# Hybrid convolution and delta-rule layer on one core: q, k, v stored by chunk, spreads by transposes, the last projection pairs product by product, early masks, longer steps for three conv norms

## The chip, the cores and the metric

The kernel runs on one core of one Trainium2 chip. The metric is the device time of one execution in microseconds (us). All engines run at once, each through its own queue in order: TensorE (PE), VectorE (DVE), ScalarE (ACT), GpSimd (POOL) and SyncE (SP), which here issues nearly all DMAs. Arithmetic is float32; large products are made from operands split into a high and a low part.

## The reference

For 1024 tokens of width 1024 the layer computes

```
h = x + 0.5 * swiglu_ffn(rmsnorm(x), ffn1)             # width 2816
u = rmsnorm(h) @ w_mix_in                              # 3 x 512 conv, q k v z of 4 heads x 128, b, a
y_conv = rmsnorm_by_group_of_64(cb * conv3(cc * ch))
q, k, v = silu(conv4(q k v));  q, k = l2norm(q), l2norm(k)
beta = sigmoid(b);  g = -exp(A_log) * softplus(a + dt_bias)
o = gated_delta_rule(q, k, v, g, beta)                 # by chunks, a triangular solve in each, a scan over chunks
y_gdn = rmsnorm(o) * silu(z)
h = h + concat(y_conv, y_gdn) @ w_mix_out
h = h + 0.5 * swiglu_ffn(rmsnorm(h), ffn2)
out = rmsnorm(h)
```

## The kernel before

Activations lie transposed: 128 channels on the partitions, 512 tokens (a half, `hf`) on the free axis. A product step `mm3` (L191) issues three matmuls of 128x128 by 128x512, high by high, high by low and low by high, into one PSUM bank, then calls `tick` (L184), which runs what was put off by `later(n, f)` until n such steps have gone by. `split` (L99) makes the two parts, the high one on ACT (L103) and the low one on DVE (L104).

The stages are the first feed-forward block, the projection to q, k and v, the mixer, and the second feed-forward block. The two blocks and the q, k, v projection use a seven-product scheme (Strassen-Winograd): a `Pair` (L323) makes two neighbouring column tiles for both halves, with products p1 and p2 in its head and p6, p5, p7, p4, p3 in `body` (L381). Each of them is 12 matmuls. p7, p4 and p3 go on in PSUM banks that p6 and p5 began, and DVE reads the bank between two of them. `all_pairs` (L426) puts the bodies of pairs 0, 1 and of pairs 2, 3 in the order product by product (p6 of one, p6 of the other, p5 of one, ...), and those of the pairs from 4 on one after the other; the q, k, v projection has six pairs, so its pairs 4 and 5 (tiles 8, 9 and 10, 11: v) come singly. Tasks have a load, a preparation and a run; preparations go 4 and loads 9 tasks ahead.

When a pair's tile is done, `conv4` (L824) makes its causal convolution over four tokens: a scaling on ACT (L826), three DVE operations (L828), a SiLU on ACT (L830), and a store to `qkv_dr` in DRAM (L831). Its second half and v tiles 10 and 11 are done in the mixer by `late_convs` (L1319): 14 convolutions, each in two steps, a load and the convolution.

The mixer has 8 chunks of 128 tokens. `build(c)` (L984) loads k and q of the chunk from `qkv_dr` (L988), makes the decay matrices by matmuls of a mask with `r0` (L993 on POOL, L1013 and L1016 on PE), and in later steps transposes k, q and v on PE by `flip` (L925, L929). v is loaded (L1050) one step ahead of its transpose (L1065). `solve(g)` (L1076) inverts the diagonal blocks of four chunks on DVE (L1094, L1098); `finish(c)` and `scan(c)` end each chunk. Between such steps `pump` (L1332) issues product steps of the z and short-convolution projections (`rest`), 2.7 for each step of a build. `drive` (L1362) runs the builds of chunks 0 to 3 three steps apart with one step of `late_convs` after each of their steps, then those of chunks 4 and 5 with three steps of `solve(0)` after each.

A conv norm (`conv_norm`, L1224) squares a finished tile, has `reduce` 7 product steps later sum it by groups of 64 (four PE matmuls, L1231, a scaling on DVE, L1234, and a power on POOL, L1237), and `scale` 8 steps after that widen the factors on ACT (L1242), spread them over the partitions by four PE matmuls with the identity (L1245) and multiply (L1247). There are 8 of them: 4 tiles by 2 halves. `Norm.spread` (L241, L245) spreads the factors of the wide norms in the same way, 7 times, and the last norm does it at L1512, in two halves. A float32 matmul of this kind is two PE instructions in the trace, a transpose is one.

The tiles `ghi`, `glo` (parts of the decay gates `gcol`), `mask`, `yfull` and `x64s` are allocated in the mixer's own pool `mx` and written at its start (L936 to L950). This pool takes the memory that the first block's temporary tiles leave. The framework may change the order of instructions within an engine's queue, except where `keep_in_program_order` pins them: it goes by program order and its own reckoning of when operands are there.

Of the kernel before, what the change touches and what calls it, by code (L numbers as in the profile page):

```python
# [57 lines left out]
def tile_hybrid(  # L58
# [122 lines left out]
    def later(n, f):  # L181
        queue.append((count[0] + n, f))
# [21 lines left out]
    class Norm:  # L204
# [36 lines left out]
        def spread(self, pinned=True):  # L241

            self.rb = psum(self.bank)
            for b in range(4):
                ins = nc.tensor.matmul(out=self.rb[:, b * P:(b + 1) * P],  # L245
                                       lhsT=self.rs[:, b:b + 1].broadcast_to([P, P]),
                                       rhs=ident, start=True, stop=True)
                tc.keep_in_program_order(ins)
            for f in self.waiting:
                f()  # L250

# [171 lines left out]
            yield run_p4, lambda: self.tsum("T4", r["B21"], t["T2"], ALU.add), lambda: self.get("B21")  # L423
            yield run_p3, lambda: self.ready("B22")

    def all_pairs(pairs, x, norm2, between={}):  # L426


        inside = pairs[EARLY:EARLY + INSIDE]

        def heads_of(some):
            for p in some:
                task(*p.head1())
                task(*p.head2())

        norm2.then(lambda: x.sums(0, norm2.rb))
        for a in (0, 2):
            products = list(zip(*(p.body() for p in pairs[a:a + 2])))
            if a == 0:

                for one, two in zip(*products[:2]):
                    task(None, one[1], one[2])
                    task(None, two[1])
                for k in range(KH):
                    task(lambda k=k: [p.both(k) for p in pairs[:2]])
                heads_of(inside[:1])
            for n, two in enumerate(products):
                if a == 0 and n == 1:

                    task(lambda: norm2.then(lambda: x.sums(2, norm2.rb)),  # L450
                         lambda: norm2.then(lambda: x.sums(1, norm2.rb)))
                if a > 0 or n > 1:
                    for t in two:
                        task(*t)
                if a == 0 and n == 2:
                    heads_of(inside[1:])
            if a in between:
                task(between[a])
        for i in range(4, len(pairs)):
            body = list(pairs[i].body())  # L460
            if EARLY + INSIDE <= i + 1 < len(pairs):
                body[2:2] = [pairs[i + 1].head1()]
                body[4:4] = [pairs[i + 1].head2()]
            for t in body:
                task(*t)
# [175 lines left out]
    with ExitStack() as stack:  # L641
# [137 lines left out]
        def ch(ap):  # L779
            return ap.rearrange("p (c e) -> p c e", e=HEADS)  # L780

        beta = small("beta")
        gcol = small("gcol")

        def gates():
# [22 lines left out]
            for n in (11, 9, 7, 5, 3, 1):  # L808
# [5 lines left out]
            nc.vector.tensor_scalar(out=gcol, in0=gcol, scalar1=-1.0, scalar2=None, op0=ALU.mult)  # L814
            nc.vector.tensor_tensor(out=ch(gcol), in0=ch(gcol),
                                    in1=ealog.unsqueeze(1).broadcast_to([P, NCH, HEADS]), op=ALU.mult)


        qkv_dr = [[dram.tile([P, HEADS, HALF], F32, name=f"qkv_dr{g}{hf}") for hf in range(NH)] for g in range(3)]

        v_dr = [dram.tile([P, HALF + 3], F32, name=f"v_dr{n}") for n in range(HEADS)]
        u_dr = [dram.tile([P, HALF + 3], F32, name=f"u_dr{n}") for n in range(12)]
# [1 line left out]
        def conv4(n, hf, u, acc):  # L824
            wc = V_GC + 4 * n
            nc.scalar.activation(out=acc, in_=u[:, 3:HALF + 3], func=AF.Copy, scale=vcol(wc + 3))  # L826
            for i in range(3):
                nc.vector.scalar_tensor_tensor(out=acc, in0=u[:, i:i + HALF], scalar=vcol(wc + i), in1=acc,  # L828
                                               op0=ALU.mult, op1=ALU.add)
            nc.scalar.activation(out=acc, in_=acc, func=AF.Silu)  # L830
            nc.sync.dma_start(out=qkv_dr[n // HEADS][hf][:, n % HEADS, :], in_=acc)  # L831

        def qkv_pair(n):
            us = {}
# [20 lines left out]

        pairs = [qkv_pair(n) for n in (4, 6, 0, 2, 8, 10)]
        early_heads(pairs[:EARLY])
        all_pairs(pairs, xm, nm[1], {0: lambda: project_ba(0), 2: lambda: project_ba(1)})


        order = [w_z[t] for t in range(HEADS)] + [w_cv[i * 4 + t] for t in range(4) for i in (1, 2, 0)]
# [21 lines left out]
    with ExitStack() as stack:  # L883
# [49 lines left out]
            return a[:, c * HEADS:(c + 1) * HEADS]  # L933


        ghi = mx.tile([P, NCH * HEADS], F32R, name="ghi")  # L936
        nc.vector.tensor_copy(out=ghi, in_=gcol)
        glo = mx.tile([P, NCH * HEADS], F32R, name="glo")
        nc.vector.tensor_tensor(out=glo, in0=gcol, in1=ghi.bitcast(F32), op=ALU.subtract)
        mask = mx.tile([P, 2 * P], F32R, name="mask")  # L940
        nc.vector.tensor_copy(out=mask[:, 0:P], in_=gt)
        nc.vector.tensor_copy(out=mask[:, P:2 * P], in_=ones)
        yfull, x64s = [], []
        for i in range(2):
            yf = mx.tile([P, HEADS * P], F32, name=f"yf{i}")
            nc.gpsimd.memset(yf, 0.0)
            yfull.append(yf)
            xs = mx.tile([64, HEADS * 64], F32, name=f"x64{i}")
            nc.gpsimd.memset(xs, 0.0)
            x64s.append(xs)  # L950

        def hd(ap):
            return ap.rearrange("p (h i) -> p h i", h=HEADS)

# [29 lines left out]
        def build(c):  # L984
            hf, ts = c // CPH, slice((c % CPH) * C, (c % CPH + 1) * C)
            qT, kT, vT = gt_tile("qT"), gt_tile("kT"), gt_tile("vT")
            for g, dst in ((1, kT), (0, qT)):
                nc.sync.dma_start(out=heads(dst), in_=qkv_dr[g][hf][:, :, ts])  # L988

            r0 = []  # L990
            for part in (ghi, glo):
# [55 lines left out]
            keep(c, "at", at)  # L1047
            yield

            nc.sync.dma_start(out=heads(vT), in_=qkv_dr[2][hf][:, :, ts])  # L1050
            pq2 = flip(qT)
            for t in range(HEADS):
                junk = mx.tile([P, P], F32, name="junk", tag="junk", bufs=1)
# [170 lines left out]
        def conv_norm(acc, t, hf):  # L1224
# [3 lines left out]
            def reduce():  # L1228
                pc2 = psum("mm")
                for b in range(4):  # L1230
                    nc.tensor.matmul(out=pc2[:, 2 * b:2 * b + 2], lhsT=sq[:, b * P:(b + 1) * P], rhs=ind2,  # L1231
                                     start=True, stop=True)
                ms = mx.tile([P, 8], F32, name="cms", tag="cms", bufs=2)
                nc.vector.tensor_scalar(out=ms, in0=pc2[:, 0:8], scalar1=1.0 / 64, scalar2=EPS,  # L1234
                                        op0=ALU.mult, op1=ALU.add)
                rs = mx.tile([P, 8], F32, name="crs", tag="crs", bufs=2)
                nc.gpsimd.tensor_tensor(out=rs, in0=ms, in1=pneg[:, 0:8], op=ALU.pow)  # L1237
                later(8, lambda: scale(rs))

            def scale(rs):  # L1240
                rw = mx.tile([P, HALF], F32, name="rw", tag="cs", bufs=3)
                nc.scalar.copy(out=rw.rearrange("p (e i) -> p e i", i=64), in_=along(rs, 64))  # L1242
                rb = psum("mm")
                for b in range(4):
                    nc.tensor.matmul(out=rb[:, b * P:(b + 1) * P], lhsT=rw[:, b * P:(b + 1) * P],  # L1245
                                     rhs=ident, start=True, stop=True)
                nc.vector.scalar_tensor_tensor(out=acc, in0=acc, scalar=vcol(V_CO + t), in1=rb,  # L1247
                                               op0=ALU.mult, op1=ALU.mult)
                nc.sync.dma_start(out=y_dr[0][hf][t // 2][:, t % 2, :], in_=acc)

            later(7, reduce)


        z_done = []
# [120 lines left out]
                yield  # L1375

        rings(qT=3, kT=3, vT=3, v=2, dec=3, kd=2, lt=2, eb=2)
        builds = pipeline([build(c) for c in range(CPH)], 3)
        drive(builds, PACE[0], late, 1)
        for _ in late:  # L1380
# [80 lines left out]
    with ExitStack() as stack:  # L1461
# [47 lines left out]
        rbs = [psum() for _ in range(2)]  # L1509
        for i in range(2):  # L1510
            for b in range(2 * i, 2 * i + 2):
                nc.tensor.matmul(out=rbs[i][:, b * P:(b + 1) * P], lhsT=rs[:, b:b + 1].broadcast_to([P, P]),  # L1512
                                 rhs=ident, start=True, stop=True)
            last[1].rb = rbs[i]
            scale_out(1, slice(2 * i * P, (2 * i + 2) * P))
        while queue:
# [66 lines left out]
```

## Time and profile before

| | |
|---|---|
| median of 3 runs | 1872.53 us (1869.71 to 1873.36) |
| the profiled execution | 1876.93 us, its span 1875.2 us |
| mean granted TensorE clock | 0.988 |
| DVE, ACT, POOL busy | 1315.6, 743.7, 733.5 us |
| DMA moved | 313.50 MB, mean 167 GB/s |

Positions are microseconds from the start of the span. In this trace the q, k, v projection ends at about 804, the mixer's products (bank `ps_mm`) follow, and the second feed-forward block begins at about 1218. Busy time of PE is the union of matmuls whose ends are modelled; the distance from one matmul's start to the next's is what one costs when PE is full. In a timeline row the columns are start, length, engine, line, operation, output<-inputs, shape, count, and in brackets the idle time before it with what ended it.

### The profile page before, as it was taken

How to read it: one execution, taken by the hardware profiler on the slowest of the kernel's cores; microseconds unless marked ns; L12 is line 12 of the kernel's file. 1: busy time of each engine (PE TensorE's matmuls, PEld its weight loads, DVE VectorE, ACT ScalarE, POOL GpSimd, SP SyncE). 2: the span in 40 equal slices, each digit the busy share in tenths (PEclk: the TensorE clock that was granted, in tenths of full speed). 3: DMA queues.
4: the chain of work that ended last, by engine and by line, in shares of the span. 5: the costliest groups of instructions: out<-in, count | busy, mean ns of one | idle time of the engine just before them, and what ended most of it. 6: DMA issues, size and time to landing. Idle time of an engine off the chain costs nothing.

```text
span 1875.2 us, 24951 instructions
## 1 busy us (share of the span) xinstructions
PE 1804.2 (96%) x8512; PEld 1476.4 (79%) x8512; DVE 1315.6 (70%) x1997; ACT 743.7 (40%) x1514; POOL 733.5 (39%) x514
## 2 busy tenths in 40 slices
PE   6899999999999999889899999999999999999997
PEld 5688888888888877677678887778888888888886
DVE  4976666667766888867767665877665666777666
ACT  6422323233534554356443343443232222344443
POOL 1474455446332434233322102045554455444243
PEclk9999999999999999999999999999999999999999
DMA  8144343436974533458754475533444334488643
GB/s 294 56 152 141 113 149 126 146 110 216 317 258 150 167 126 118 135 186 265 234 157 151 120 264 176 182 105 102 142 134 146 107 132 150 145 288 286 213 132 99
DMA packets 196240, 313.50 MB, mean 167 GB/s; under 512 B 28048, under 2 KB 50576, under 8 KB 196112
## 3 DMA queue, kind: packets, MB, share of 16 engines
q1 hardware_dynamic: 192656, 306.60, 49.5%
q10 hardware_dynamic: 3456, 5.31, 0.9%
q8 instruction: 67, 1.10, 0.2%
q14 instruction: 61, 0.50, 0.1%
HBM read 228.97 MB, written 82.86 MB: 166 GB/s over the span
## 4 chain that ended last, share of the span: by engine, by line
PE 79%; DVE 10%; DMA 4%; issue 2%; ACT 2%; POOL 2%; SPq 1%; ACTq 0%; POOLq 0%; DVEq 0%
PE ps_ps L192 23%; PE ps_ps L194 23%; PE ps_ps L193 22%; PE ps_mm L192 2%; PE ps_mm L194 2%; PE ps_mm L193 2%; DVE wlo L104 2%; DVE lo L104 2%; PE ps_aux L923 1%; DVE cv L828 1%; DMA gd<-qkv_dr 1%; DMA raw<-w_in 1%; DVE sv L1094 1%; DVE xb L1098 1%; DVE h L304 0%
## 5 line engine op out<-in xcount | busy, mean ns | idle before, releaser
L192 PE MATMUL ps_ps<-hi,whi 128*128 128x512 f32 x1400 | 550.6, 394 | 13.5 <-ACT p L353 2.8
L194 PE MATMUL ps_ps<-hi,wlo 128*128 128x512 f32 x1400 | 548.6, 392 | 5.9 <-DVE wlo L104 5.9
L193 PE MATMUL ps_ps<-lo,whi 128*128 128x512 f32 x1400 | 549.0, 392 | 2.9 <-DVE lo L104 2.9
L104 DVE TENSOR_TENSOR wlo<-T,whi 128x512 fp32r<-128x512 f32 x244 | 229.4, 954 | 138.7 <-ACT whi L103 137.9
L104 DVE TENSOR_TENSOR wlo<-raw,whi 128x512 fp32r<-128x512 f32 x280 | 255.0, 922 | 100.9 <-ACT whi L103 99.9
L192 PEld LDWEIGHTS ps_ps<-hi,whi 128*128 128x128 f32 x1400 | 265.0, 189 | 76.1 <-issue 5.7
L111 POOL TENSOR_TENSOR T<-raw 128x512 f32<-128x512 f32 x144 | 227.3, 1579 | 228.9 <-DMA raw<-w_out 90.1
L194 PEld LDWEIGHTS ps_ps<-hi,wlo 128*128 128x128 f32 x1400 | 265.0, 189 | 63.6 <-DVE wlo L104 8.1
L193 PEld LDWEIGHTS ps_ps<-lo,whi 128*128 128x128 f32 x1400 | 265.1, 189 | 59.9 <-DVE lo L104 5.5
L192 PE MATMUL ps_ps<-ghi,whi 128*128 128x512 f32 x616 | 241.3, 392 | 0.0
L194 PE MATMUL ps_ps<-ghi,wlo 128*128 128x512 f32 x616 | 240.7, 391 | 0.4 <-DVE wlo L104 0.4
L193 PE MATMUL ps_ps<-glo,whi 128*128 128x512 f32 x616 | 240.6, 391 | 0.0
L103 ACT CAST whi<-raw 128x512 fp32r<-128x512 f32 x280 | 169.0, 617 | 61.8 <-DMA raw<-w_in 23.8
L103 ACT CAST whi<-T 128x512 fp32r<-128x512 f32 x244 | 146.1, 616 | 70.6 <-POOL T L111 33.2
L104 DVE TENSOR_TENSOR glo<-raw,ghi 128x512 fp32r<-128x512 f32 x154 | 129.6, 842 | 46.9 <-ACT ghi L103 44.1
L192 PE MATMUL ps_mm<-hi,whi 128*128 128x512 f32 x384 | 159.9, 416 | 0.9 <-DVE u L417 0.9
L194 PE MATMUL ps_mm<-hi,wlo 128*128 128x512 f32 x384 | 152.9, 398 | 0.0
L193 PE MATMUL ps_mm<-lo,whi 128*128 128x512 f32 x384 | 151.9, 395 | 0.0
L194 PEld LDWEIGHTS ps_ps<-ghi,wlo 128*128 128x128 f32 x616 | 115.7, 188 | 26.7 <-DVE wlo L104 1.2
L193 PEld LDWEIGHTS ps_ps<-glo,whi 128*128 128x128 f32 x616 | 115.9, 188 | 25.3
L192 PEld LDWEIGHTS ps_ps<-ghi,whi 128*128 128x128 f32 x616 | 115.8, 188 | 25.3
L111 POOL TENSOR_TENSOR T<-raw,T 128x512 f32<-128x512 f32 x50 | 72.6, 1452 | 159.1 <-DMA raw<-w_in 131.1
(223 smaller groups left out, 2250.7 us busy)
## 6 DMA issues: line engine op xcount, KB each, us to landing
raw<-w_in SPq DMA_DIRECT2D x264, 256.0 KB, 4.5
raw<-w_out SPq DMA_DIRECT2D x154, 256.0 KB, 4.2
raw<-w_qkv SPq DMA_DIRECT2D x36, 256.0 KB, 3.7
f1S<-S SPq DMA_DIRECT2D x33, 256.0 KB, 4.8
raw<-f1A SPq DMA_DIRECT2D x33, 256.0 KB, 3.8
raw<-f1S SPq DMA_DIRECT2D x33, 256.0 KB, 3.6
f2S<-S SPq DMA_DIRECT2D x33, 256.0 KB, 4.7
raw<-f2A SPq DMA_DIRECT2D x33, 256.0 KB, 4.8
```

The source lines that it names most:

```text
L103: tc.keep_in_program_order(nc.scalar.copy(out=hi, in_=src))
L104: nc.vector.tensor_tensor(out=lo, in0=src, in1=hi.bitcast(F32), op=ALU.subtract)
L111: tc.keep_in_program_order(nc.gpsimd.tensor_tensor(out=out, in0=in0, in1=in1, op=op))
L192: nc.tensor.matmul(out=ps, lhsT=whi, rhs=xhi, start=start, stop=False, skip_group_check=True)
L193: nc.tensor.matmul(out=ps, lhsT=whi, rhs=xlo, start=False, stop=False, skip_group_check=True)
L194: nc.tensor.matmul(out=ps, lhsT=wlo, rhs=xhi, start=False, stop=stop, skip_group_check=True)
L828: nc.vector.scalar_tensor_tensor(out=acc, in0=u[:, i:i + HALF], scalar=vcol(wc + i), in1=acc, op0=ALU.mult, op1=ALU.add)
L923: nc.tensor.matmul(out=ps[:, sl], lhsT=lhs[:, sl], rhs=rhs[:, sl], start=start, stop=stop)
L1094: nc.vector.tensor_tensor(out=tv, in0=lrow[:, lo:hi].unsqueeze(2).broadcast_to([nb, n, j + 1]), in1=xrow[:, 0:j + 1].unsqueeze(1).broadcas ...
L1098: nc.vector.tensor_tensor(out=xv, in0=xv, in1=tv, op=ALU.subtract)
```

## The change

- `qkv_dr` is laid out by chunk, [4 chunks, 128, 4 heads, 128 tokens], so that a chunk's load reads 2 KB in one run for each partition in place of four runs of 512 B, and the store of `conv4` writes four runs of 512 B in place of one of 2 KB.
- v of a chunk is loaded together with its k and q, and four steps of `late_convs` (the convolutions of v tiles 10 and 11, first half) are issued ahead of the first build.
- All spreads are PE transposes in place of matmuls with the identity.
- Pairs 4 and 5 of the q, k, v projection go product by product too.
- `ghi`, `glo`, `mask`, `yfull`, `x64s` lie in the pool `const`, which lives as long as the kernel, and are written in the early part of the program; `ghi` and `glo` at the end of `gates`, which follows `project_ba(1)`.
- The conv norms of tiles 0 to 2 have 10 steps ahead of `reduce` and 16 ahead of `scale`; tile 3 keeps 7 and 8.

```diff
 def spread(self, pinned=True):
-                ins = nc.tensor.matmul(out=self.rb[:, b * P:(b + 1) * P],
-                                       lhsT=self.rs[:, b:b + 1].broadcast_to([P, P]),
-                                       rhs=ident, start=True, stop=True)
-                tc.keep_in_program_order(ins)
+                tc.keep_in_program_order(
+                    nc.tensor.transpose(out=self.rb[:, b * P:(b + 1) * P],
+                                        in_=self.rs[:, b:b + 1].broadcast_to([P, P]), identity=ident))
...
-    def all_pairs(pairs, x, norm2, between={}):
+    def all_pairs(pairs, x, norm2, between={}, twos=(0, 2)):
-        for a in (0, 2):
+        for a in twos:
-        for i in range(4, len(pairs)):
+        for i in range(twos[-1] + 2, len(pairs)):
...
+        ghi, glo = (const.tile([P, NCH * HEADS], F32R, name=n) for n in ("ghi", "glo"))
+        mask = const.tile([P, 2 * P], F32R, name="mask")
+        nc.vector.tensor_copy(out=mask[:, 0:P], in_=gt)
+        nc.vector.tensor_copy(out=mask[:, P:2 * P], in_=ones)
+        yfull, x64s = [], []
...
             nc.vector.tensor_tensor(out=ch(gcol), in0=ch(gcol),
                                     in1=ealog.unsqueeze(1).broadcast_to([P, NCH, HEADS]), op=ALU.mult)
+            nc.vector.tensor_copy(out=ghi, in_=gcol)
+            nc.vector.tensor_tensor(out=glo, in0=gcol, in1=ghi.bitcast(F32), op=ALU.subtract)
...
-        qkv_dr = [[dram.tile([P, HEADS, HALF], F32, name=f"qkv_dr{g}{hf}") for hf in range(NH)] for g in range(3)]
+        qkv_dr = [[dram.tile([CPH, P, HEADS, C], F32, name=f"qkv_dr{g}{hf}") for hf in range(NH)] for g in range(3)]
...
-            nc.sync.dma_start(out=qkv_dr[n // HEADS][hf][:, n % HEADS, :], in_=acc)
+            nc.sync.dma_start(out=qkv_dr[n // HEADS][hf][:, :, n % HEADS, :].rearrange("c p i -> p c i"),
+                              in_=acc.rearrange("p (c i) -> p c i", c=CPH))
...
-        all_pairs(pairs, xm, nm[1], {0: lambda: project_ba(0), 2: lambda: project_ba(1)})
+        all_pairs(pairs, xm, nm[1], {0: lambda: project_ba(0), 2: lambda: project_ba(1)}, (0, 2, 4))
...
-            for g, dst in ((1, kT), (0, qT)):
-                nc.sync.dma_start(out=heads(dst), in_=qkv_dr[g][hf][:, :, ts])
+            for g, dst in ((1, kT), (0, qT), (2, vT)):
+                nc.sync.dma_start(out=heads(dst), in_=qkv_dr[g][hf][c % CPH])
...
-            nc.sync.dma_start(out=heads(vT), in_=qkv_dr[2][hf][:, :, ts])
             pq2 = flip(qT)
...
-                later(8, lambda: scale(rs))
+                later(16 if t < 3 else 8, lambda: scale(rs))
...
-                    nc.tensor.matmul(out=rb[:, b * P:(b + 1) * P], lhsT=rw[:, b * P:(b + 1) * P],
-                                     rhs=ident, start=True, stop=True)
+                    nc.tensor.transpose(out=rb[:, b * P:(b + 1) * P], in_=rw[:, b * P:(b + 1) * P], identity=ident)
...
-            later(7, reduce)
+            later(10 if t < 3 else 7, reduce)
...
+        for _ in range(4):
+            next(late)
         builds = pipeline([build(c) for c in range(CPH)], 3)
...
-                nc.tensor.matmul(out=rbs[i][:, b * P:(b + 1) * P], lhsT=rs[:, b:b + 1].broadcast_to([P, P]),
-                                 rhs=ident, start=True, stop=True)
+                nc.tensor.transpose(out=rbs[i][:, b * P:(b + 1) * P], in_=rs[:, b:b + 1].broadcast_to([P, P]),
+                                    identity=ident)
```

More of the change, by code (lines that the diff above doesn't have):

```diff
@@ L780, in ch @@
             return ap.rearrange("p (c e) -> p c e", e=HEADS)
+        ghi, glo = (const.tile([P, NCH * HEADS], F32R, name=n) for n in ("ghi", "glo"))
[3 more added lines that the diff above has]
+        yfull, x64s = [], []
+        for i in range(2):
+            yf = const.tile([P, HEADS * P], F32, name=f"yf{i}")
+            nc.gpsimd.memset(yf, 0.0)
+            yfull.append(yf)
+            xs = const.tile([64, HEADS * 64], F32, name=f"x64{i}")
+            nc.gpsimd.memset(xs, 0.0)
+            x64s.append(xs)
         beta = small("beta")
@@ L933, in cols @@
             return a[:, c * HEADS:(c + 1) * HEADS]
[L936 to L950, printed above, removed]
         def hd(ap):
```

## The prediction

> **What bounds the kernel now.** I read the page first, then PE's waits, the stretches around the mixer, and the timelines of PE, SP and DVE at each wait. The page says which engine sets the time:
>
> ```profile
> PE 1804.2 (96%) x8512; PEld 1476.4 (79%) x8512; DVE 1315.6 (70%) x1997; ACT 743.7 (40%) x1514; POOL 733.5 (39%) x514
> ```
>
> PE is busy for 96% of the span, so there are two ways to gain: fewer PE instructions, or less waiting in the 71 us (1875.2 less 1804.2) that are left. PE's waits (total, times, longest, in us) name the causes:
>
> ```profile
> PE ps_aux L929 <- DMA gd<-qkv_dr: 10.9, 4, 3.6
> ...
> PE ps_ps L192 <- DVE u L397: 2.4, 1, 2.4
> PE ps_ps L192 <- DVE c L406: 2.3, 2, 2.1
> PE ps_aux L1013 <- POOL r L993: 2.3, 2, 1.3
> ```
>
> The stretches of the end of the q, k, v projection and the first part of the mixer (columns: stretch, its length, busy us of PE, weight loads, DVE, ACT, POOL, then granted clock, DMA share, GB/s) show a second cost, a clock below 1:
>
> ```profile
> 770.00:805.00 35.00, 29.36 (x118) 22.12 (x117) 24.73 (x59) 11.29 (x21) 3.05 (x3) 0.95 0.33 114
> 805.00:825.00 20.00, 17.71 (x89) 14.47 (x88) 15.87 (x27) 13.79 (x34) 9.66 (x11) 1.00 0.65 210
> 825.00:845.00 20.00, 16.93 (x81) 14.24 (x80) 13.79 (x25) 12.19 (x30) 6.28 (x6) 0.91 0.72 231
> 845.00:865.00 20.00, 17.64 (x85) 14.79 (x84) 14.39 (x26) 13.92 (x35) 7.38 (x6) 0.91 0.89 280
> 865.00:885.00 20.00, 18.08 (x89) 15.13 (x89) 15.98 (x25) 13.42 (x35) 7.72 (x7) 0.91 0.79 249
> 885.00:905.00 20.00, 16.38 (x73) 13.25 (x72) 11.67 (x29) 11.38 (x31) 5.71 (x5) 0.91 0.80 241
> 905.00:925.00 20.00, 20.00 (x110) 16.95 (x109) 18.79 (x59) 7.74 (x28) 8.22 (x7) 1.00 0.72 227
> 925.00:950.00 25.00, 20.65 (x94) 17.15 (x93) 19.99 (x58) 6.28 (x19) 7.04 (x5) 0.86 0.71 230
> ```
>
> Each stretch with a PE wait of some 2 us or more also has a lowered clock, and those without have 1.00. A wait therefore costs its idle time and, where the clock falls, the missing clock: 0.09 of 20 us is 1.8 us.
>
> **The change part by part.** *Spreads by transposes.* A spread by matmuls, and the next instruction's start; then a group of four transposes, and the next start:
>
> ```profile
> 618.80 1.05 PE L245 MATMUL ps_ps<-cs,rs 128*128 128x128 f32 x8
> 619.61 0.47 PE L192 MATMUL ps_ps<-ghi,whi 128*128 128x512 f32 x1
> ```
>
> ```profile
> 866.18 0.60 PE L929 MATMUL ps_aux<-cs,gd 128*128 128x128 f32 x4
> 866.54 0.48 PE L192 MATMUL ps_mm<-hi,whi 128*128 128x512 f32 x1
> ```
>
> Four matmuls are eight instructions and take 0.81 us; four transposes take 0.36. There are 7 wide spreads, 8 of the conv norms and the two halves of the last norm, 16 groups: 16 x 0.45 = 7.2 us. PE is full around nearly all of them, or something waits for the result, so I count the whole; the low end is 5, if DVE is what ends last at some of them.
>
> *Pairs 4 and 5 product by product.* In the single pair 5, p7 and p4 go on in a bank that DVE has to read first, and the next product has nothing else ahead of it:
>
> ```profile
> 791.38 0.47 PE L192 MATMUL ps_ps<-hi,whi 128*128 128x512 f32 x1 [2.38 <-DVE u L397]
> 791.69 0.40 PE L193 MATMUL ps_ps<-lo,whi 128*128 128x512 f32 x1
> 791.92 0.40 PE L194 MATMUL ps_ps<-hi,wlo 128*128 128x512 f32 x1
> ```
>
> With two pairs a product of the other lies between: 12 matmuls at the 0.23 us from row to row above, 2.8 us, more than the 2.38 here and the 2.1 of `c` L406. Both go, 4.5 us, and the missing clock of 770 to 805, 0.05 x 35 = 1.8 us. Against this the first-half convolutions of tiles 8 and 9, six DVE operations of this length,
>
> ```profile
> 785.42 0.75 DVE L828 SCALAR_TENSOR_TENSOR cv<-u,vs,cv 128x512 f32<-128x512 f32 x1
> ...
> 809.14 1.52 DVE L937 CAST ghi<-gcol 128x32 fp32r<-128x32 f32 x1 [0.67 <-DVE wlo L104]
> ```
>
> 4.5 us in all, move from before pair 5 to the very end of the projection. They may queue ahead of DVE's last read of the banks, which the mixer's first product waits for. I set 1.8 us against it, some two and a half of the six. That leaves 4.5 us (1.8, with all six ahead, to 6.3).
>
> *Early masks.* The casts of `ghi` and `mask` come only at 809.14 (row above), and PE's two waits for `r0`, 2.3 us, follow from them. With `ghi` ready by the end of the gates POOL makes `r0` while PE is still in the products. All 2.3 us go (0 to 2.3: the slots of `r0` still have to come free). At the kernel's start the moved clears and casts lie on POOL and DVE beside loads and first products; I count them at nothing, and 1 us if DVE has them ahead of a first split.
>
> *v with k and q.* Chunk 0's v was asked for here, when PE was all but there:
>
> ```profile
> 829.39 0.52 SPq L1050 DMA_DIRECT2D gd<-qkv_dr  x1
> ```
>
> and a load takes 4.2 us to land, a store of a convolution 2.9:
>
> ```profile
> qkv_dr<-cv SPq DMA_DIRECT2D x24, 256.0 KB, 2.9
> gd<-qkv_dr SPq DMA_DIRECT2D x24, 256.0 KB, 4.2
> ```
>
> One step of a build is 2.7 product steps of three matmuls, 2.7 x 3 x 0.23 = 1.9 us and some small ones, so asking one step ahead can't cover 4.2 us; asking with k, five steps ahead, covers it. Three of the four DMA waits are for v (chunks 0 to 2) and go: 10.9 - 3.6 = 7.3 us, and the clock with them, 3 x 1.8 = 5.4 us. The longest, 3.6, is for k of chunk 4, which SP issues behind a store of chunk 3's v:
>
> ```profile
> 894.26 0.32 SPq L981 DMA_DIRECT2D st_v<-gd  x1
> 894.68 1.23 SPq L988 DMA_DIRECT2D gd<-qkv_dr  x2
> ```
>
> The change doesn't touch that order. It may shrink, since `late_convs` is done four steps sooner and DVE is freer: 1 us (0 to 5.4, with its clock). The 512-byte runs only go from loads to stores, as many as before; by the two DMA rows I expect loads nearer 2.9 and stores nearer 4.2 us, with neither end of this below PE's slack. Sum: 7.3 + 5.4 + 1 = 13.7 us. The added wait is of chunk 0's v load: it needs the stores of convolutions 10 and 11. While SP stands there, the weight loads, the stores of chunk 0 and k and q of chunk 1 stand behind it; two units of weights are loaded ahead, which PE works on meanwhile, so I count it at 1 to 2 us, within the new stalls below.
>
> *Longer steps for conv norms.* PE waits here for a widened factor:
>
> ```profile
> 926.54 1.05 PE L1231 MATMUL ps_mm<-cs,sq 128*128 128x2 f32 x8
> ...
> 937.49 1.90 PE L1245 MATMUL ps_mm<-cs,rw 128*128 128x128 f32 x8 [4.32 <-ACT rw L1242]
> ```
>
> ```profile
> 933.97 0.15 DVE L1234 TENSOR_SCALAR cms<-ps_mm 128x8 f32<-128x8 f32 x1
> ...
> 955.17 0.18 DVE L1098 TENSOR_TENSOR xb<-xb,sv 64x31 f32<-64x31 f32 x1
> ```
>
> The sum left PE at 926.5, and DVE, in the middle of `solve(0)`, scaled it only at 934. From the sum to the spread were 11 us; 8 more product steps at 0.69 us are 5.5, more than the 4.3 of idle time. Idle time and clock (0.14 x 25 = 3.5) make 7.8 us. But DVE's chain of `solve(0)` ends at 955.17 and PE needs its result in `finish(0)`. DVE is busy 80% of this stretch and 94% of the one before, so PE can run ahead of it only while it has other products. I take 5 (2 to 7.8).
>
> *New stalls.* From 805 to 905 DVE is busy 71.7 us (sum of the five rows). Without some 19 us of waits and clock the stretch is 81 us and DVE's share 88%. In the stretch with 80 to 94% one queued DVE step cost PE 4.3 us and its clock. I charge one such, 6 us (0 to 18: three).
>
> Sum: 7.2 + 4.5 + 2.3 + 13.7 + 5 - 6 = 26.7, say 27 us. Against the profiled execution, 1876.9 (span 1875.2), that is 1850; this one lies 4.4 us above the median of the runs shown, 1872.5, so the timed median should be about 1846.
>
> [...] The shortest wait that led to a slow clock ended in transposes:
>
> ```profile
> 876.04 0.88 PE L929 MATMUL ps_aux<-cs,gd 128*128 128x128 f32 x4 [1.92 <-DMA gd<-qkv_dr]
> ...
> 878.85 0.63 PE L192 MATMUL ps_mm<-hi,whi 128*128 128x512 f32 x1
> 879.28 0.59 PE L193 MATMUL ps_mm<-lo,whi 128*128 128x512 f32 x1
> ```
>
> After 1.92 us of idle time matmuls follow each other at 0.43 us, while after 2.38 us ahead of ordinary matmuls, at 791, they kept 0.23. So transposes may keep the clock down; the rows alone don't settle it, and by them a spread's clock term is nothing. [...]
>
> **The rivals.** (1) Another engine or the DMAs become the bound in the compressed mixer. For it: DVE at 88 to 94%, and DMA share up to 0.89 at 280 GB/s. Against: PE lost nothing at 94% between 905 and 925. Three new stalls in place of one give 27 - 12 = 15 us, 1858. (2) Everything comes and nothing new does: 27 + 6 + 2.8 = 36 us, 1837. (3) Idle time goes, the clock doesn't: spreads now are transposes, and what is left of a wait counts longer. Clock terms 1.8 + 5.4 and the part taken of 3.5, some 9 us, stay: 1855. (4) The framework orders the queue so that v still comes late, and the change doesn't do what it says: without 12.7 us, 1859. (5) Slower: SP stands at v. PE wanted k of chunk 1 here:
>
> ```profile
> 825.63 0.60 PE L929 MATMUL ps_aux<-cs,gd 128*128 128x128 f32 x4
> ```
>
> If chunk 0's v load sits right behind k and q and holds SP until 829.4, as late as it went before, k of chunk 1, issued after it (0.5) and 4.2 us on the way, lands at 834.1, and PE idles 8.5 us with 1.8 of clock. The same happens at chunk 4, behind the last convolution (three DVE steps of 0.75, its store 2.9, a load 4.2: 9.4 us and 1.8), and at chunk 7, whose v has a single buffer (a load, 4.2 us, and 1.8): 27.5 us in all. The rest of the gain, without chunk 0's v (a third of 12.7) and without the 1 us for chunk 4, is 21.5, so this loses 6: 1878.5. It decides from 21.5 us of standing. Against it: convolutions 10 and 11 lay behind other work in the trace, and now they are issued first.
>
> **How the numbers follow.** Forecast 1846, its own range 1839 to 1854, chance 0.6. Rival 1: 0.15; rival 2: 0.1; rival 3: 0.05; rival 4: 0.04; rival 5: 0.04; 0.02 for a smaller gain or none. The range takes in rivals 1 to 4 with most of the unknown ends: 1833 to 1862. About 0.2% (3.7 us) is what a measurement of this kernel can tell from no change. Faster: 0.93; same 0.03; slower 0.04.
>
> **What would show it.** Right: L245, L1245 and L1512 with half the instructions; no PE wait for `u` L397, `c` L406 or `r` L993; waits for `qkv_dr` down from 10.9 to under 4 us; clock 1.00 from 825 to 885 and in the conv norms' stretch; the first feed-forward block unchanged. Wrong: PE waits for DVE (L1023, L1032, `wlo`) or for weights that add up to over 6 us between the mixer's start and the end of `solve(0)`; SP idle at L988; a clock below 1 without a wait; or the end of the mixer not earlier although its beginning is.

## The result, and the profile after

The changed kernel takes 1862.43 us (median of 5 runs, 1860.39 to 1865.06) against 1873.21 for the kernel before on the same chip (1869.71 to 1874.74). The ratio is 0.9942, 95% interval [0.9928, 0.9956]: faster by 10.9 us, 8 to 13.5. The forecast was 27 us. The profiled execution took 1864.1 us, span 1862.4, mean granted clock 0.989 (before: 1876.9, 1875.2, 0.988). First the engines' row of its page:

```profile
PE 1793.7 (96%) x8448; PEld 1464.3 (79%) x8448; DVE 1304.6 (70%) x1997; ACT 751.3 (40%) x1520; POOL 731.4 (39%) x514
```

PE has 64 instructions fewer, as 16 groups of eight turned into groups of four must give. Its busy time fell by 10.5 us (1804.2 to 1793.7); 7.2 of these are what the spreads were to save, and busy time also holds what a low clock adds to the matmuls (0.42 us from one to the next in place of 0.23 after 692.89, below). Its idle time, span less busy, fell only from 71.0 to 68.7 us. That is most of the result in one line: the work went, the waiting stayed. Now PE's waits (total, times, longest, us):

```profile
PE ps_ps L194 <- DVE wlo L104: 9.3, 6, 3.8
PE ps_aux L944 <- DMA gd<-qkv_dr: 3.4, 2, 2.8
...
PE ps_mm L192 <- ACT whi L103: 2.7, 1, 2.7
PE ps_aux L964 <- DMA xc<-diag_x: 2.6, 1, 2.6
PE ps_mm L1229 <- ACT sq L1224: 2.3, 1, 2.3
```

The waits for `u` L397, `c` L406 and `r` L993 are gone, the one for v and k is 3.4 us in place of 10.9, and the 4.3 us for the widened factor `rw` are 0.2. Others stand in their place: for a weight's low part (9.3 us in place of 6.2), for its high part, for the result of the triangular solve on its way through DRAM, for a conv norm's square. The stretches show where (columns as before; the mixer now starts at 801.6):

```profile
767.00:802.00 35.00, 32.52 (x144) 24.53 (x143) 29.29 (x68) 13.86 (x25) 8.31 (x7) 1.00 0.41 130
802.00:822.00 20.00, 17.34 (x73) 13.80 (x72) 14.02 (x24) 12.49 (x27) 0.41 (x1) 0.91 0.77 229
822.00:842.00 20.00, 19.35 (x110) 16.36 (x109) 15.58 (x26) 18.62 (x41) 11.78 (x9) 1.00 0.92 289
842.00:862.00 20.00, 18.04 (x95) 14.77 (x94) 12.70 (x26) 16.56 (x43) 9.13 (x7) 1.00 0.99 310
862.00:882.00 20.00, 17.40 (x87) 14.06 (x88) 16.68 (x33) 16.65 (x38) 7.70 (x6) 1.00 0.81 258
...
922.00:947.00 25.00, 20.14 (x89) 15.76 (x87) 20.77 (x61) 5.66 (x11) 5.07 (x3) 0.93 0.45 145
947.00:972.00 25.00, 22.25 (x169) 18.42 (x170) 12.84 (x36) 17.44 (x63) 8.24 (x7) 0.88 0.59 178
```

The end of the projection is as forecast (32.5 of 35 us busy against 29.4, clock 1.00). From 822 to 882 the clock is back at 1.00. But PE still idles 0.7 to 2.6 us in each of those three, and the clock is low in new ones: 802 to 822 and 922 to 972. DVE's share stayed far under the 88% that the prediction worked out: 74% over the 100 us from 802, against 72% over those from 805 before. The DMA share rose to 0.92 and 0.99 from 822 to 862, and the only wait of PE for a DMA there is 0.65 us. In the two profiled executions the changed kernel is 3.2 us ahead at the mixer's first product (804.73 to 801.58), 12.4 at the second feed-forward block's first product (1217.87 to 1205.52) and 12.8 at the end.

Of the signs that the prediction named for being right, all that lie in the projection and the mixer's beginning came, but not the clock in the conv norms' stretch (0.93 and 0.88). One that it named for being wrong came too: PE's waits for DVE and weights between the mixer's start and the end of `solve(0)`, 2.66, 1.07, 1.55, 0.98 and 0.87 us among them, pass 6 us.

### The profile page after: what moved, and what is told of

It reads as the page before. It is cut to its first block, busy times and chain, and to the rows that moved or that the text cites. A ratio compares the mean times of both kernels' runs of the same rounds, so it can differ in the third digit from the quotient of the medians.

```text
span 1862.4 us, 24801 instructions
## 1 busy us (share of the span) xinstructions
PE 1793.7 (96%) x8448; PEld 1464.3 (79%) x8448; DVE 1304.6 (70%) x1997; ACT 751.3 (40%) x1520; POOL 731.4 (39%) x514
## 4 chain that ended last, share of the span: by engine, by line
PE 78%; DVE 10%; ACT 4%; DMA 3%; issue 3%; POOL 1%; SPq 0%; ACTq 0%; POOLq 0%; DVEq 0%
PE ps_ps L194 22%; PE ps_ps L192 22%; PE ps_ps L193 22%; PE ps_mm L192 2%; PE ps_mm L194 2%; PE ps_mm L193 2%; DVE wlo L104 2%; DVE lo L104 1%; PE ps_aux L938 1%; DMA raw<-w_in 1%; DVE cv L842 1%; DVE sv L1092 1%; DVE xb L1096 1%; ACT whi L103 1%; DVE h L303 1%
## 5 line engine op out<-in xcount | busy, mean ns | idle before, releaser
L192 PE MATMUL ps_ps<-hi,whi 128*128 128x512 f32 x1400 | 550.1, 394 | 10.6 <-ACT hi L103 3.2
L192 PEld LDWEIGHTS ps_ps<-hi,whi 128*128 128x128 f32 x1400 | 264.7, 189 | 72.0 <-ACT whi L103 4.7
L111 POOL TENSOR_TENSOR T<-raw 128x512 f32<-128x512 f32 x144 | 222.8, 1548 | 234.8 <-DVE wlo L104 102.5
L192 PE MATMUL ps_ps<-ghi,whi 128*128 128x512 f32 x616 | 241.3, 392 | 0.0
L192 PE MATMUL ps_mm<-hi,whi 128*128 128x512 f32 x384 | 159.8, 416 | 3.8 <-ACT whi L103 2.7
L192 PEld LDWEIGHTS ps_ps<-ghi,whi 128*128 128x128 f32 x616 | 115.7, 188 | 25.3
```

Source lines behind the costliest of these rows:

```text
L111: tc.keep_in_program_order(nc.gpsimd.tensor_tensor(out=out, in0=in0, in1=in1, op=op))
L192: nc.tensor.matmul(out=ps, lhsT=whi, rhs=xhi, start=start, stop=False, skip_group_check=True)
```

## The experiments

Every kernel ran beside the kernel before, on several chips, so kernels are compared by their ratios to it: microseconds are 1873 times (1 less the ratio), and the difference of two kernels has the two intervals taken together (root of the sum of squares). The theories, in the names that the expectations use: **Q**, a part that removes a wait brings a wait of its own by turning the order in some engine's queue; **B**, each part gains in full alone, and together DVE runs out; **C**, the end of `solve(0)` on DVE caps the mixer; **D**, early v costs as much as it gives.

**One part alone on the kernel before.** `a_spreads`, `b_pairs`, `c_v`, `d_masks` and `e_norms` each take one part of the diff above and nothing else; `c_v` holds the layout, the early load and the four late steps.

```diff
 a_spreads, at all three places
-                ins = nc.tensor.matmul(out=self.rb[:, b * P:(b + 1) * P],
...
+                    nc.tensor.transpose(out=self.rb[:, b * P:(b + 1) * P],
```

> Only the spreads by transposes, on the kernel before. Theory Q (each part brings its own new wait by changing the order in the queues): PE saves 16 x 0.45 = 7.2 us, but DVE takes the sums of the second mixer norm ahead of a weight split and PE waits some 3.8 us with a slow clock of 1.7 us near 692, so the gain is 2 to 3.5 us. Theory B (parts gain in full alone; together DVE runs out in the mixer): 6 to 7 us faster and no wait near 692.

Measured: 1871.97 us, ratio 0.9997 [0.9989, 1.0006]: nothing. Its page against that of before (PE 1804.2, x8512, idle 71.0):

```profile
PE 1797.0 (96%) x8448; PEld 1467.0 (78%) x8448; DVE 1314.8 (70%) x1997; ACT 743.8 (40%) x1514; POOL 731.5 (39%) x514
```

PE's busy time fell by the 7.2 us of the forecast, and its idle time rose by 6.9, to 77.9 (span 1874.9). The gain, 0.6 us (-1.1 to 2.1), is less than even Q expected. In PE's waits those for `qkv_dr` have grown from 10.9 to 14.4 us, and one long wait is in its timeline where the kernel before had 1.14 us:

```profile
692.51 0.80 PE L194 MATMUL ps_ps<-hi,wlo 128*128 128x512 f32 x1 [3.92 <-DVE wlo L104]
```

```diff
 b_pairs
-        all_pairs(pairs, xm, nm[1], {0: lambda: project_ba(0), 2: lambda: project_ba(1)})
+        all_pairs(pairs, xm, nm[1], {0: lambda: project_ba(0), 2: lambda: project_ba(1)}, (0, 2, 4))
```

> Only pairs 4 and 5 product by product, on the kernel before. Both theories: the two waits of 2.4 and 2.1 us and the slow clock near 800 go, 4 to 6 us earlier at the start of the mixer. Q: most of it is there at the end too (3 to 6 us faster). B: less than 2 us at the end, because the mixer gives it back.

Measured: 1866.12 us, 0.9966 [0.9954, 0.9978]: 6.4 us (4.1 to 8.6), where the prediction had 4.5 (1.8 to 6.3). In its trace the mixer starts at 797.55 in place of 804.73.

```diff
 c_v
-            for g, dst in ((1, kT), (0, qT)):
-                nc.sync.dma_start(out=heads(dst), in_=qkv_dr[g][hf][:, :, ts])
+            for g, dst in ((1, kT), (0, qT), (2, vT)):
+                nc.sync.dma_start(out=heads(dst), in_=qkv_dr[g][hf][c % CPH])
...
+        for _ in range(4):
+            next(late)
```

> Only v with k and q, the layout by chunk, and four steps of the late convolutions ahead of the builds, on the kernel before. Q: the three waits for v go (7.3 us and 5.4 us of clock), and this part itself makes a new wait of PE for a z weight split behind the convolutions on ACT (2.7 us and 1.7 us of clock) and smaller waits for DVE; 4 to 8 us faster. B: 10 to 14 us faster.

Measured: 1868.4 us, 0.9978 [0.9967, 0.999]: 4.1 us (1.9 to 6.2) of 13.7. From the list of PE's waits:

```profile
PE ps_aux L930 <- DMA gd<-qkv_dr: 3.7, 2, 2.0
...
PE ps_mm L192 <- ACT whi L103: 2.0, 1, 2.0
```

```diff
 d_masks
+            nc.vector.tensor_copy(out=ghi, in_=gcol)
+            nc.vector.tensor_tensor(out=glo, in0=gcol, in1=ghi.bitcast(F32), op=ALU.subtract)
...
-        ghi = mx.tile([P, NCH * HEADS], F32R, name="ghi")
```

> Only the masks and cleared tiles in the constant pool and early, on the kernel before. Q and B: PE's two waits for r0 go, 2.3 us; between 0 and 3 us faster. If the moved casts cost at the kernel's start, the first 100 us are longer by up to 1 us.

Measured: 1876.02 us, 1.0016 [1.0007, 1.0024]: 3 us slower (1.3 to 4.5). The waits for `r0` are gone. At the last pairs the wait for `c` grew from 2.3 to 3.3 us, and the one of 2.4 us, for `u` before, now ends with the cast of `ghi`, which stands in DVE's queue among the pairs' reads:

```profile
PE ps_ps L192 <- DVE c L406: 3.3, 1, 3.3
...
PE ps_ps L192 <- DVE ghi L830: 2.4, 1, 2.4
```

The mixer begins 1.3 us later (806.0 in place of 804.73). That is not the whole 3 us: the profiled execution, 1873.48 us, is faster than the median, so the rest isn't seen in a trace.

```diff
 e_norms
-                later(8, lambda: scale(rs))
+                later(16 if t < 3 else 8, lambda: scale(rs))
...
-            later(7, reduce)
+            later(10 if t < 3 else 7, reduce)
```

> Only the longer steps of three conv norms, on the kernel before. Both: the wait of 4.3 us at 937 and its slow clock go. Q: another wait of 2 us or more with a slow clock comes within 40 us behind it (for the square on ACT, or for xc), and the gain is 0 to 4 us. Full gain, 5 us or more with no new wait, speaks against Q.

Measured: 1874.91 us, 1.0006 [0.9995, 1.0017]: 1.1 us slower, within the interval. The 4.3 us at `rw` went; 16 us later PE stood for the solve instead, and a low clock followed (PE's timeline, then a stretch):

```profile
953.49 0.59 PE L965 MATMUL ps_aux<-xc,gd 32*32 32x32 f32 x16 [2.33 <-DMA xc<-diag_x]
```

```profile
954.80:968.50 13.70, 13.70 (x81) 11.91 (x80) 6.15 (x19) 6.51 (x23) 3.30 (x3) 0.50 0.15 44
```

The five parts alone add up to 6.4 + 4.1 + 0.6 - 3.0 - 1.1, 7 us; together they give 10.9. B falls with this: only the pairs gain in full alone.

**One part undone in the changed kernel.** In `f_nm1` the spread of `nm[1]`, the norm ahead of the q, k, v projection, goes by matmuls again; the other 15 groups stay transposes.

```diff
+                    nc.tensor.matmul(out=self.rb[:, b * P:(b + 1) * P], lhsT=col_, rhs=ident, start=True, stop=True)
+                    if self.by_matmul else
...
+        nm[1].by_matmul = True
```

> The changed kernel, with the spread of the second mixer norm alone by matmuls again (+0.45 us of PE). Theory Q (the wait near 692 comes from DVE's order alone): DVE takes both weight splits ahead of the sums again, the wait of 3.8 us there falls to about 1.2 us and the slow clock near 693 goes; 3 to 5 us faster than the changed kernel, some 1858 to 1860. Theory C (the solve on DVE caps what the mixer can give, so what is won ahead of it is lost at its end): within 1.5 us of the changed kernel, 1861 to 1864.

Measured: 1857.58 us, 0.9916 [0.9903, 0.9929]: 4.9 us faster than the change itself (3.6 on either side), with four PE instructions more. DVE's timeline of the changed kernel shows why; `h` L302 and L303 are the sums that make the projection's operands (L306 and L307 in `f_nm1`), `wlo` is a weight's low part:

```profile
675.43 0.68 DVE L104 TENSOR_TENSOR wlo<-raw,whi 128x512 fp32r<-128x512 f32 x1
678.36 1.29 DVE L302 TENSOR_TENSOR h<-h,ps_ps 128x512 f32<-128x512 f32 x2 [2.25 <-ACT rb L739]
...
690.48 0.68 DVE L104 TENSOR_TENSOR lo<-h,hi 128x512 fp32r<-128x512 f32 x1
691.08 1.75 DVE L104 TENSOR_TENSOR wlo<-raw,whi 128x512 fp32r<-128x512 f32 x1
```

and PE's at the same place:

```profile
688.68 0.39 PE L193 MATMUL ps_ps<-lo,whi 128*128 128x512 f32 x1
692.89 0.60 PE L194 MATMUL ps_ps<-hi,wlo 128*128 128x512 f32 x1 [3.82 <-DVE wlo L104]
693.29 0.63 PE L192 MATMUL ps_ps<-hi,whi 128*128 128x512 f32 x1
693.71 0.63 PE L193 MATMUL ps_ps<-lo,whi 128*128 128x512 f32 x1
```

In `f_nm1` one more weight split stands ahead of the sums, right after one at 675.93:

```profile
678.61 0.70 DVE L104 TENSOR_TENSOR wlo<-raw,whi 128x512 fp32r<-128x512 f32 x1 [1.99 <-ACT whi L103]
679.37 1.29 DVE L306 TENSOR_TENSOR h<-h,ps_ps 128x512 f32<-128x512 f32 x2
```

In the changed kernel the sums stand ahead of that split, presumably because the shorter spread makes them ready sooner by the framework's reckoning. The split then comes 12.5 us later (691.08 against 678.61), behind 14 DVE operations, and PE waits for it: 3.82 us in place of 1.10, with a clock that falls (matmuls 0.42 us apart in place of 0.23). The sums themselves start only 1.0 us sooner (678.36 against 679.37).

`a2_spreads_nm1` asks the same on the kernel before: the spreads alone, that of `nm[1]` by matmuls.

> The kernel before with the spreads by transposes, that of nm[1] kept by matmuls, and nothing else. If the turned order of DVE's queue at nm[1] is what ate the gain of the spreads: no wait for wlo near 692, no slow clock there, and 4 to 6 us below the kernel before (14 or 15 spreads of 0.45 us, and 0.5 to 1 given back), against 1 us for all spreads. If the shorter spreads are worth nothing because another engine ends last at them: within 1.5 us of the kernel before.

Measured: 1867.38 us, 0.9963 [0.9949, 0.9976]: 6.9 us (4.5 to 9.6), against 0.6 for all 16. Fifteen groups at 0.45 are 6.75. With PE's busy time 8.2 us lower and idle time 1.0 us higher the page agrees (busy 1796.0, span 1868.0, idle 72.0), and so does the timeline, where the wait is the old size:

```profile
PE 1796.0 (96%) x8452; PEld 1465.9 (78%) x8452; DVE 1306.8 (70%) x1997; ACT 743.0 (40%) x1514; POOL 736.5 (39%) x514
```

```profile
692.63 0.50 PE L194 MATMUL ps_ps<-hi,wlo 128*128 128x512 f32 x1 [1.15 <-DVE wlo L104]
```

So Q holds at this place, shown twice: one group of four instructions costs 4.9 us in the changed kernel and 6.3 on the kernel before (6.9 less 0.6), each with some 3 to 3.6 us on either side. That it is the order of the queues, and not the transposes, is in the traces; why the framework turns it is not shown.

`g_nomask` is the change without the early masks, `h_nov` without everything that concerns v (layout, load, late steps).

```diff
 g_nomask
-            nc.vector.tensor_copy(out=ghi, in_=gcol)
...
 h_nov
-            for g, dst in ((1, kT), (0, qT), (2, vT)):
+            for g, dst in ((1, kT), (0, qT)):
...
-        for _ in range(4):
-            next(late)
```

> The changed kernel without the early masks (they are in the mixer's pool again). If the early masks alone cost 3 us on the kernel before by chance of the clock's phase, they are worth their 2.3 us here and this is 1 to 3 us slower than the changed kernel, 1863 to 1866. If they really displace something (theory Q), it is as fast or up to 3 us faster, 1859 to 1863.

> The changed kernel without the part on v: old layout, v one step ahead, no late convolutions in front. Q: the part is worth here what it was worth alone (5 us), so 1866 to 1869, the waits for qkv_dr are back, and the wait of 2.7 us for a weight split at 816 is gone. C: within 2 us of the changed kernel, since solve(0) caps both.

Measured: 1861.7 us, 0.9935 [0.9922, 0.9948], and 1862.54 us, 0.9943 [0.9931, 0.9955]. Both are as fast as the change itself: neither part is worth anything that these runs can tell, and Q's 1866 to 1869 for `h_nov` was wrong. In `h_nov` the waits for `qkv_dr` are back,

```profile
PE ps_aux L943 <- DMA gd<-qkv_dr: 10.9, 5, 2.8
```

7.5 us more than in the change, and still it is as fast. Its trace lacks the changed kernel's wait for `whi` at 815.90 (2.7 us), and its wait for `xc` is 1.2 us in place of 2.6. The mixer's first 100 us show the exchange, first in the change, then in `h_nov`:

```profile
802.00:902.00 100.00, 91.81 (x459) 75.22 (x458) 73.79 (x149) 75.30 (x181) 36.97 (x29) 0.98 0.89 276
```

```profile
802.00:902.00 100.00, 91.91 (x467) 76.66 (x467) 76.99 (x152) 70.85 (x178) 38.28 (x30) 0.98 0.84 268
```

PE is idle 8.2 us in one and 8.1 in the other, at the same clock. In `h_nov` these are four waits for `qkv_dr` (2.56, 1.35, 2.44, 1.74 us); in the change one of 0.65 us is left, and the other 7.5 us are waits for ACT and DVE.

**What caps the mixer.** `j_short` is the change, and `k_short_nov` is `h_nov`, both without rows 8 to 30 of the 31 rows of `solve(0)`: its result is then incomplete. The solve's own DVE operations take 8.8 us in `j_short` in place of 29.0, 20 us less (all of DVE's busy time is 14.4 us less, 1304.6 to 1290.2).

```diff
-            for j in range(BLK - 1):
+            for j in range(BLK - 1 if g else BLK // 4):
```

> The changed kernel with 23 of the 31 rows of solve(0) left out (part of the computation is missing; it is run for its time). Theory C (the end of solve(0) on DVE holds PE at the first use of xc): the wait of 2.6 us for xc and the slow clock behind it go, and 4 us or more are won. If other work holds PE there, under 2 us.

> The changed kernel without the part on v, with the same rows left out. C: with the solve out of the way the part on v shows its worth, and this kernel is 4 to 8 us slower than the one with v early and the same rows left out. Theory D (v early costs as much as it gives, because four convolutions go ahead of the first build on ACT and DVE): the two are within 2 us of each other.

Measured: 1853.07 us, 0.9887 [0.9867, 0.9907], and 1853.09 us, 0.9886 [0.9866, 0.9906]: 10.3 and 10.7 us below their own full kernels by the ratios. `solve(0)` does cost time, about half of the DVE time of the operations left out. But with it out of the way early v still shows no gain (it loses 0.2 us, with 5.3 on either side, where C expected 4 to 8), and C, as far as it was to explain where v's gain went, is not borne out.

In `l_v0late` (`f_nm1` without the late steps ahead, chunk 0's v asked for one step ahead as before) and `m_nov_nm1` (`h_nov` with the spread of `nm[1]` by matmuls) D is put to the test.

```diff
 l_v0late
-            for g, dst in ((1, kT), (0, qT), (2, vT)):
+            for g, dst in ((1, kT), (0, qT)) + (((2, vT),) if c else ()):
...
-        for _ in range(4):
-            next(late)
```

> The changed kernel with the second mixer norm's spread by matmuls, v with k and q from chunk 1 on, chunk 0's v one step ahead of its transpose as before, and no late convolutions ahead of the builds. D: the wait of 2.7 us for a weight split at the mixer's start goes, the first store of diagonal blocks comes 17 to 19 us after the mixer's start in place of 26, one wait for chunk 0's v of some 3 us stays; 1 to 4 us faster than the same kernel with the convolutions ahead (1857.6). C: within 1.5 us of it.

> The changed kernel with the second mixer norm's spread by matmuls and without the part on v. C and D: as fast as the same with v early, 1856 to 1860. If v early is worth its 5 us once the wait near 692 is gone, 1862 or more.

Measured: `l_v0late` 1861.08 us, 0.9929 [0.9913, 0.9945]; `m_nov_nm1` 1858.61 us, 0.9919 [0.9902, 0.9936]. The first is not faster than `f_nm1` but, if anything, slower (by 2.4 us of the ratios, 3.9 on either side): taking the four late steps away, with chunk 0's v late again, gains nothing, so D, which puts v's cost on these steps, is not borne out either. The second equals `f_nm1` within the intervals: again v is worth nothing. Three pairs of kernels differ by v alone (the change and `h_nov`, `k_short_nov` and `j_short`, `f_nm1` and `m_nov_nm1`), and by the ratios v gains 0.2 us, loses 0.2 and gains 0.6, with 3.4, 5.3 and 4.0 us on either side.

`n_min` leaves v, masks and longer steps out at once: the kernel before with the pairs and with the spreads of `a2_spreads_nm1`.

> The kernel before with the pairs product by product and the spreads by transposes, that of nm[1] kept by matmuls; nothing of v, of the layout, of the early masks, of the longer conv norm steps. Theory D, extended (early v, early masks and longer steps give back in the mixer what they take out): as fast as the kernel of the change with nm[1] by matmuls, 1857 to 1860 us. Theory B (each of these parts gains something that needs the others): 1862 to 1866 us, that is the pairs' 6.4 us and 2 to 4 for the spreads. The sum of the prediction without those parts: 1873 less 7.2 less 4.5, 1861 to 1862 us.

Measured: 1861.23 us, 0.9938 [0.9925, 0.9951]: 11.6 us, about the sum of `b_pairs` and `a2_spreads_nm1` (6.4 + 6.9 = 13.3). It lies between the theories' numbers, and on the prediction's own sum for these two parts (1861 to 1862). `f_nm1` is 4.1 us below it, with 3.4 us on either side. So two small edits make the whole time of the change, and the other three parts add some 4 us when the nm[1] spread is kept out of their way. `m_nov_nm1`, which has masks and steps without v, is 3.6 us below `n_min`, with 4.0 on either side: what is added may lie in masks and steps, but these runs don't show it.

`f_nm1`, at 1857.58 us, is the fastest of the full kernels.

## Why the prediction was wrong

The direction was right and the size was not: 10.9 us in place of 27, with 1862.4 just past the upper end of the range.

**Spreads, 7.2.** The cost from the two rows (0.81 and 0.36 us) was right: PE's busy time fell by 7.2 in `a_spreads`, and the pair L246 and L192 in the changed kernel shows 0.36:

```profile
618.08 0.60 PE L246 MATMUL ps_ps<-cs,rs 128*128 128x128 f32 x4
618.44 0.47 PE L192 MATMUL ps_ps<-ghi,whi 128*128 128x512 f32 x1
```

"I count the whole" holds for 15 groups (6.9 measured) and fails for one, the spread of `nm[1]`, which costs 4.9 in the changed kernel and so leaves about 2 of the 7.2. The prediction looked at what waits for a spread, and not at what its earlier end moves in DVE's queue.

**Pairs, 4.5.** Right in mechanism, 6.4 measured, and 4.5 lies within its interval; the charge of 1.8 for convolutions queued at the end was at any rate not too low. What there is of it shows as a wait of 1.18 us at the mixer's first product (0.88 before).

**Masks, 2.3, and norm steps, 5.** Each wait that was named went, and alone neither gained: masks lost 3.0, steps 1.1 (within the interval). With the rest in place the two together give about 3.6 of 7.3, with 4.0 on either side. At the norm steps the prediction's own doubt came true, that PE "can run ahead of it only while it has other products". DVE's last row of the solve, SP's load and PE's wait in the changed kernel:

```profile
942.42 0.18 DVE L1096 TENSOR_TENSOR xb<-xb,sv 64x31 f32<-64x31 f32 x1
```

```profile
942.63 0.47 SPq L1100 DMA_DIRECT2D diag_x<-xb  x1
944.89 0.37 SPq L1111 DMA_DIRECT2D xc<-diag_x  x1
```

```profile
946.98 0.59 PE L964 MATMUL ps_aux<-xc,gd 32*32 32x32 f32 x16 [2.59 <-DMA xc<-diag_x]
```

The solve's result goes out to DRAM and back, 4.4 us from the end of DVE's row to PE's start, and PE now stands for it.

**v with k and q, 13.7.** The waits went as worked out, 7.5 us of them, and the clock from 822 to 882 is back at 1.00. The loads took 3.8 us to land in place of 4.2 and the stores 3.3 in place of 2.9, the way that was expected but not as far. The gain is 4.1 alone and, with the rest in place, none: the three pairs of kernels average 0.2 us, with 2.5 us on either side. The waits themselves were no firm figure: with v left as before they came to 5.9 us in `b_pairs`, 9.7 in `d_masks` and 14.4 in `a_spreads`, against the 10.9 that the sum was built on. What stands in their place is partly to be seen. At 815.9 a split of weights on ACT came behind two SiLUs of the late convolutions that were put ahead:

```profile
812.72 0.63 ACT L844 ACTIVATE cv<-cv 128x512 f32<-128x512 f32 x1 [1.23 <-DVE cv L842]
813.27 0.60 ACT L1272 ACTIVATE s<-ps_mm 128x512 f32<-128x512 f32 x1
814.70 0.63 ACT L844 ACTIVATE cv<-cv 128x512 f32<-128x512 f32 x1 [0.83 <-DVE cv L842]
815.24 1.12 ACT L103 CAST whi<-raw 128x512 fp32r<-128x512 f32 x2
```

PE waited 2.66 us for that cast, and the clock fell (0.52 from 815.90 to 819.30). This is the row that the prediction lacked: it put the wait on SP's queue alone, and ACT's stood as well. But `l_v0late`, which takes the four steps away, loses the wait and is no faster: others come (2.7 us for v at 824.97, 3.2 for ACT at 903.03, 3.9 for `xc` at 942.24). So this wait alone did not take the gain. What is seen is the exchange in the first 100 us, 8.1 us of waits for `qkv_dr` against 0.65 for it and 7.5 for ACT and DVE. That DVE's `solve(0)` costs time behind them is shown (10.3 us for 20 us less of it); that the builds' DVE and ACT work as a whole paces this part, which would make any one wait there worthless, is only argued. Why the exchange is so even, and v therefore worth nothing, stays open.

**New stalls, 6 (0 to 18).** This is the step that failed: the sum took each removed wait as worth its whole length and its clock, and set one new stall against all of them. Without the charge the sum was 27 + 6 = 33 us and the gain is 10.9, so 22 us are missing, outside the term's bounds. By the parts above 13.5 of them are v's (13.7 against 0.2), 5 the spread of `nm[1]`, some 4 masks and steps, and the pairs gave 2 more than their term: 20 to 21, with several us of uncertainty. The 5 came outside the mixer, from a place where nothing was looked for; the rest came in the mixer, in waits for ACT (815.9), for DVE and for the solve's way through DRAM. The charge rested on DVE's share, which said little: it was 74% over the 100 us from 802, with all these waits in it.

**From 1850 to 1846.** The gain was read in an execution that lay 4.4 us above the median, and was then taken off the median in full. That holds only if an execution of median time has all the losses that were read in this one. From one profiled execution to the other the gain is 12.8 us (1876.9 to 1864.1), 1.9 more than the timed one.

**The rivals.** The first, new stalls for 12 more, named what happened most nearly, and was itself too small; its ground, that DVE or the DMAs become the bound, does not show in their shares. Rival 2 fell. Rival 3 fell where it was looked for (clock 1.00 from 822 to 882). Rival 4 fell: v is issued ahead. Rival 5 stood on a real wait, which did not decide: SP held chunk 0's v load until 819.70 and issued k of chunk 1 at 824.45,

```profile
819.70 0.32 SPq L987 DMA_DIRECT2D gd<-qkv_dr  x1
...
824.45 0.38 SPq L987 DMA_DIRECT2D gd<-qkv_dr  x1
```

and PE stood only 0.65 us for it at 829.39.

## What to carry to other kernels

Don't take a wait on the profile as worth its length until you have looked at what PE would wait for next, in every queue; when several are to be removed in one stretch, charge a new one for each, and test each part alone and undone, since here two small edits (`n_min`) made as much as the whole change. When an operation gets shorter, compare the order of the neighbouring engines' queues before and after: a framework that orders by readiness may move other work, and one spread saved 0.45 us and cost 5. Span less busy time, before and after, tells in one subtraction whether waits were removed or only moved; what the low clock added here (matmuls 0.42 us apart in place of 0.23) is in the busy time.

## What the runs showed of the hardware

In the changed kernel the low clock came in stretches of about 3.4 us. The granted clock, the third figure from the right, is 0.51 or 0.52 in four of these rows and 1.00 in the two that stand ahead of a fall:

```profile
815.90:819.30 3.40, 3.40 (x8) 2.72 (x9) 3.18 (x7) 1.61 (x3) 0.00 (x0) 0.52 1.04 302
926.40:928.60 2.20, 2.18 (x14) 1.97 (x15) 2.11 (x8) 1.48 (x3) 1.76 (x1) 1.00 0.87 298
928.60:932.00 3.40, 3.40 (x10) 2.62 (x9) 3.13 (x9) 0.00 (x0) 0.00 (x0) 0.51 0.88 277
947.00:949.00 2.00, 2.00 (x43) 1.55 (x43) 0.99 (x4) 1.91 (x7) 0.00 (x0) 1.00 0.40 73
949.00:952.50 3.50, 3.50 (x20) 2.61 (x17) 1.34 (x5) 3.27 (x13) 0.93 (x1) 0.52 0.08 14
969.50:973.00 3.50, 3.50 (x18) 2.46 (x16) 0.00 (x0) 3.13 (x14) 0.00 (x0) 0.52 0.84 288
```

After the waits that ended at 926.42 and 946.98 PE ran some 2 us at full clock before it fell. The starts, about 815.9, 928.6, 949.0 and 969.5, lie 112.7, 20.4 and 20.5 us apart, 33, 6 and 6 times 3.40 to 3.42. A wait that was followed by such a stretch so cost some 1.6 us more, by an estimate from these rows: 0.48 of 3.4. Not every wait was followed by one: in the kernel before the clock stayed at 1.00 after the 2.38 us of idle time that ended at 791.38, and was 0.50 from 797.8 to 801.2 after the 2.15 us that ended at 796.53. What makes the difference no run here shows. The low clock also lasted longer: in `e_norms` it was 0.50 for 13.7 us (row above), four times 3.4, while PE was busy throughout with transposes, masks' matmuls, matmuls of 128x128 and blocks of 32x32 and 64x64, and with only three matmuls of an ordinary product. That would fit the prediction's guess that transposes may keep the clock down, but no run here separates them from the other matmuls.
